# Seven products for eight in a transformer step: layer 1's up projection by Strassen's algorithm

## The chip, the cores and the metric

The kernel runs on one core of a Trainium2 chip. The metric is the device time in microseconds; the time before is the median of three runs. Beside the runs there is one profiled execution, whose trace gives the rows below.

## The reference, cut to what matters

Two layers of a decoder are run once over a prompt of 512 tokens and a sample group of 8 x 4 tokens, 544 columns in all. Layer 0 mixes by a Conformer convolution, layer 1 by a state-space layer; each layer then has cross-attention to a memory and an MLP with squared relu. The change is in the MLP of layer 1 and in what stands at its two ends.

```
def _sqrelu_mlp(xn, w_up, w_down):          # w_up (1024, 4096), w_down (4096, 1024)
    h = jax.nn.relu(jnp.einsum('bld,df->blf', xn, w_up))
    return jnp.einsum('blf,fd->bld', h * h, w_down)
...
    x = x + _sqrelu_mlp(_rmsnorm(x, p['norm_ffn'][i]), p['mlp_w_up'][i], p['mlp_w_down'][i])
y = _rmsnorm(x, p['norm_final'])
```

All inputs and outputs are float32.

## The kernel before, in words

The residual stream lies in eight tiles `X[k]` of 128 features by 544 columns. A float32 product is made of three products of reduced-precision parts (`float32r`): each operand is split into a high part, rounded by ScalarE (a copy), and a low part, the difference, made by VectorE. `split` does so for activations, `prep_block` (line 163) for a weight block of 128 x 1024; the three passes are high by high, low by high and high by low. Each pass of one 128 x 128 weight tile runs over the 544 columns in two matmuls of 272 (`gemm`, line 193, matmul at line 208).

The whole trunk is a list of `Step`s. `run` (line 137) goes through it, and each engine gets its instructions in the order in which the code issues them. Ahead of a step, `run` asks for weight blocks (512 KB each) on SP's queue into the staging tiles `wst`, up to `ahead` blocks in advance, and prepares the parts of blocks to come in the three tiles `whl`. PSUM's first six banks serve as three pairs (`mm`, handed out by `ring`), the last two as `aux`.

In layer 1, `att_layer` ends with the output projection: `ofirst` and `ofin` run the products of output tile o, `oend` adds them to `X[o]` and splits the normed tile into `xf` (`norm_in`). The root mean square is not applied there: it is applied, squared, to the results of the down products (`rb`).

`mlp_layer` works by halves of the 4096 middle features. `up(o)` makes one middle tile from one weight block, 48 matmuls, then relu and square on ScalarE and the split into a high and a low tile, of which VectorE makes the low one. After 16 such tiles, `dn(half, o, c)` makes the eight output tiles, two weight blocks each, scales them by `rb` and adds them to `X[o]` (lines 1085 and 1086). In the second half the squares for the final norm are summed as well. The last output tile is made in `finish`, by halves of the columns, so that the final norm of the first half runs beside the products of the second.

Of the kernel before, what the change touches and what calls it, by code (L numbers as in the profile page):

```python
# [57 lines left out]
class Trunk:  # L58
    NST, NHL, NSLOT = 4, 3, 48
# [12 lines left out]
    def __init__(self, nc, tc, pool, psum, I, O):  # L72
# [10 lines left out]
        self.whl = deque(t(f"whl{i}", 2, 1024) for i in range(self.NHL))  # L83
        self.acc = t("acc", T)
        self.rb = t("rb", T)
        self.tmps = deque(t(f"tmp{i}", T) for i in range(2))
        self.accs = t("accs", 1, 128)
# [263 lines left out]
    def start(self):  # L351
# [46 lines left out]
        self.ahead = self.NST - 1  # L398
# [97 lines left out]
    def conv_layer(self):  # L496
# [72 lines left out]
        def end():  # L569
            self.ahead = self.NST  # L570
            self.unhold(self.vb)
# [218 lines left out]
    def att_layer(self, L, bg):  # L790
# [225 lines left out]
        def ofirst():  # L1016
            for k in (6, 7):
# [22 lines left out]
    def mlp_layer(self, L, after, bg):  # L1040
# [54 lines left out]
        for half in range(2):  # L1095
            self.steps += [up(16 * half + i) for i in range(16)]
            last = L == half == 1
            self.steps += [dn(half, o, c) for o in range(8 - last) for c in range(2)]
            if last:
                self.steps.append(Step(lambda: self.finish(M["h"]), [("dn", 1, 7, c) for c in (2, 3)]))  # L1100


    def finish(self, hs):
        nc, V = self.nc, self.nc.vector
        k = KT - 1
        col = lambda t, c: t[:, c * HALF : c * HALF + HALF]
        taus = lambda v, c: [v[:, f, :, 2 * c : 2 * c + 2] for f in range(2)]
        rows = lambda t: t.rearrange("p (j r) -> p j r", r=32)[:, :, :8].rearrange("p j (f t) -> p f j t", f=2)
        ps = [self.ring(self.mm)[:, 0, :HALF] for _ in range(2)]
        sq, own = self.slot(), self.slot()[:, :128]  # L1110
        xs = [self.slot() for _ in range(KT)]
        nc.gpsimd.memset(own, 0.0)  # L1112
        seq = [(c, i, wi, xi) for c, g in ((0, range(8)), (1, range(7)), (1, (7,)))
               for wi, xi in ((0, 0), (1, 0), (0, 1)) for i in g]

        def products(c, a=0, b=len(seq)):
            for n, (half, i, wi, xi) in enumerate(seq):
                if a <= n < b:
                    nc.tensor.matmul(ps[c], self.w8(("dn", 1, k, 2 + half), i)[wi], col(hs[8 * half + i][xi].bitcast(F32R), c),
                                     start=n == 0, stop=n == len(seq) - 1)  # L1120
# [9 lines left out]
        def others():  # L1130

            for f in range(2):
                V.tensor_copy(rows(self.accs[:, 0])[:, f], self.smp(self.acc)[:, f])
            for c in range(2):
# [39 lines left out]
        for _ in r0:  # L1174
            pass
# [673 lines left out]
```

## Time and profile before

| | |
|---|---|
| median of three runs | 1566.04 us (1563.89 to 1566.91) |
| the profiled execution | 1566.66 us, span in the trace 1564.9 us |
| TensorE busy | 1521.7 us, 97% of the span |
| VectorE busy | 897.2 us, 57% |
| ScalarE busy | 620.9 us, 40% |
| mean granted TensorE clock | 0.99 |
| layer 1's MLP without the closing step | 1163.7 to 1536.3 us of the span |

Busy time of an engine is the time in which one of its instructions runs; matmuls are pipelined, so that a busy TensorE says that matmuls follow each other, not that each is at its fastest. [...]

### The profile page before, as it was taken

Reading aid. Unit: us, or ns where it says so; the run is one execution under the profiler, and the core shown is the slowest. Engines: PE = TensorE matmul, PEld = TensorE weight load, DVE = VectorE, ACT = ScalarE, POOL = GpSimd, SP = SyncE. Lnnn points to the kernel's source line nnn. Section 1 sums busy time; section 2 is a strip of 40 time slices with the busy share of each in tenths; the row PEclk is TensorE's granted clock in tenths of the full one; section 3 lists DMA queues with packets and bytes.
Section 4 is the critical chain, followed back from the end, with each engine's and each line's share of the span. In section 5 each row is a group of like instructions: output and inputs, shape, how many; then the busy total and the mean of one; then the engine's idle time right before and its main releaser. Section 6 shows DMA issues by size and latency. Waiting matters only on the chain.

```text
span 1564.9 us, 29123 instructions
## 1 busy us (share of the span) xinstructions
PE 1521.7 (97%) x12129; PEld 1475.6 (94%) x12129; DVE 897.2 (57%) x1771; ACT 620.9 (40%) x1090; POOL 195.2 (12%) x155
## 2 busy tenths in 40 slices
PE   8999989999999999999999999999999999999996
PEld 8999869988999999999998899988899999999996
DVE  6997876444577666666757954454453333332334
ACT  6121354333445433665434443343435421244222
POOL 2445561000000000000104840000000000000001
PEclk9999989999999999999999999999999999999998
DMA  7433433663322444444588965355322222223211
GB/s 274 121 96 97 145 105 122 232 212 122 110 81 91 143 132 132 132 132 139 177 271 253 322 190 188 116 197 197 129 86 95 81 95 94 83 81 95 88 62 58
DMA packets 90804, 218.18 MB, mean 139 GB/s; under 512 B 12304, under 2 KB 42784, under 8 KB 86576
## 3 DMA queue, kind: packets, MB, share of 16 engines
q1 hardware_dynamic: 87440, 211.06, 41.2%
q10 hardware_dynamic: 3168, 5.18, 0.9%
q8 instruction: 95, 1.56, 0.4%
q14 instruction: 37, 0.30, 0.1%
q0 software_dynamic: 64, 0.08, 0.0%
HBM read 186.48 MB, written 29.80 MB: 138 GB/s over the span
## 4 chain that ended last, share of the span: by engine, by line
PE 81%; DVE 11%; DMA 3%; issue 1%; POOL 1%; ACT 1%; SPq 0%; DVEq 0%; POOLq 0%; ACTq 0%
PE banks L208 68%; DVE banks L695 2%; PE banks L460 2%; DMA arena_att<-in_kc 2%; PE banks L885 2%; PE banks L220 1%; DVE whl L170 1%; PE banks L869 1%; PE banks L675 1%; PE banks L443 1%; PE banks L949 1%; DVE banks L1577 1%; POOL arena_mem L648 1%; DMA arena_s<-tab 1%; PE banks L280 1%
## 5 line engine op out<-in xcount | busy, mean ns | idle before, releaser
L208 PE MATMUL banks<-slot,whl 128*128 128x272 f32 x9240 | 1178.0, 289 | 3.3 <-ACT slot L134 2.0
L208 PEld LDWEIGHTS banks<-slot,whl 128*128 128x128 f32 x9240 | 1167.0, 188 | 7.9 <-issue 4.1
L170 DVE TENSOR_TENSOR whl<-wst,whl 128x1024 fp32r<-128x1024 f32 x213 | 263.9, 1242 | 158.0 <-ACT whl L134 153.8
L134 ACT ACTIVATE whl<-wst 128x1024 fp32r<-128x1024 f32 x232 | 243.7, 1053 | 176.4 <-PE banks L208 105.1
L243 DVE TENSOR_TENSOR slot<-tmp,slot 128x544 fp32r<-128x544 f32 x64 | 46.4, 726 | 164.4 <-ACT slot L134 164.4
L134 ACT ACTIVATE slot<-banks 128x512 fp32r<-128x512 f32 (+7 forms) x132 | 60.4, 481 | 139.2 <-PE banks L208 42.0
L134 ACT ACTIVATE tmp<-banks 128x544 f32<-128x544 f32 x64 | 40.0, 625 | 178.1 <-PE banks L208 178.1
L134 ACT ACTIVATE slot<-x,vec 128x544 fp32r<-128x544 f32 (+2 forms) x49 | 35.0, 736 | 115.9 <-DVE x L1013 47.3
L1085 DVE TENSOR_TENSOR tmp<-banks,rb 128x544 f32<-128x544 f32 x31 | 22.5, 724 | 83.3 <-PE banks L208 83.2
L695 DVE SCALAR_TENSOR_TENSOR banks<-slot,vec,banks 128x512 f32<-128x512 f32 x90 | 67.9, 754 | 2.6
L1112 POOL MEMSET slot<- 128x128 f32 x1 | 0.2, 206 | 525.7 <-PE banks L208 525.7
L134 ACT ACTIVATE tmp<-x 128x544 f32<-128x544 f32 x41 | 26.6, 648 | 86.3 <-DVE x L1086 71.8
L675 PE MATMUL banks<-slot,arena_mem 128*128 128x128 f32 (+2 forms) x360 | 46.1, 285 | 7.2 <-POOL arena_mem L648 4.0
L170 POOL TENSOR_TENSOR whl<-wst,whl 128x1024 fp32r<-128x1024 f32 x19 | 46.2, 2437 | 55.5 <-ACT whl L134 55.5
L418 POOL TENSOR_TENSOR slot<-slot,slot 128x512 fp32r<-128x512 f32 x4 | 6.1, 1563 | 371.4 <-ACT slot L134 371.4
L675 PEld LDWEIGHTS banks<-slot,arena_mem 128*128 128x128 f32 x360 | 44.2, 200 | 8.0 <-POOL arena_mem L648 4.6
L648 POOL TENSOR_TENSOR arena_mem<-istk,slot 128x1152 f32<-128x1152 f32 x20 | 46.1, 2307 | 31.4 <-PE banks L675 27.9
L246 DVE SCALAR_TENSOR_TENSOR slot<-x,vec,slot 128x544 fp32r<-128x544 f32 x40 | 30.9, 784 | 27.0 <-ACT slot L134 26.2
L134 ACT ACTIVATE arena_prep<-arena_prep 64x64 f32<-64x64 f32 (+4 forms) x176 | 43.6, 260 | 2.8 <-DVE arena_prep L1362 1.2
L134 ACT ACTIVATE slot<-tmp 128x544 fp32r<-128x544 f32 x64 | 42.2, 660 | 2.0
L134 ACT ACTIVATE tmp<-tmp 128x544 f32<-128x544 f32 x64 | 42.2, 659 | 2.0
L134 ACT ACTIVATE slot<-banks,sm_nb,sm_rs 128x256 f32<-128x256 f32 x40 | 22.0, 563 | 43.5 <-DVE sm_nb L891 43.5
(238 smaller groups left out, 1344.3 us busy)
## 6 DMA issues: line engine op xcount, KB each, us to landing
wst<-in_w SPq DMA_DIRECT2D x231, 512.0 KB, 3.5
arena_att<-in_kc SPq DMA_DIRECT2D x16, 1024.0 KB, 7.0
arena_att<-in_vc SPq DMA_DIRECT2D x16, 1024.0 KB, 6.4
tab<-arena_prep SPq DMA_DIRECT2D x24, 512.0 KB, 5.3
arena_s<-tab SPq DMA_DIRECT2D x8, 768.0 KB, 5.6
arena_s<-tab SPq DMA_DIRECT2D x8, 512.0 KB, 6.6
arena_s<-tab SPq DMA_DIRECT2D x12, 256.0 KB, 5.7
x<-in_x SPq DMA_DIRECT2D x8, 272.0 KB, 6.0
```

What stands on the lines that cost most here:

```text
L134: self.nc.scalar.activation(out, in_, func, **kw)
L170: eng.tensor_sub(t[:, 1].bitcast(F32R), src, t[:, 0])
L208: self.nc.tensor.matmul(ps[:, c, :HALF], w, x[:, c * HALF : c * HALF + HALF], start=first and n == 0, stop=last and n == len(seq) - 1)
L220: self.nc.tensor.matmul(ps[:, c, :HALF], self.w8(b, kt)[wi], rhs[kt][xi].bitcast(F32R)[:, c * HALF : c * HALF + HALF], start=first and kt ...
L243: self.nc.vector.tensor_sub(l.bitcast(F32R), src_h if src_l is None else src_l, h)
L246: self.nc.vector.scalar_tensor_tensor(l.bitcast(F32R), src_h, scale, h, op0=ALU.mult, op1=ALU.subtract)
L460: nc.tensor.matmul(ps[m], self.memt(2 * kp + k2, xi)[:, m * 128 : m * 128 + 128], t[:, wi, k2 * 512 : k2 * 512 + 512], start=kp == 0 and k ...
L648: nc.gpsimd.tensor_mul(mat(n).rearrange("p (n c) -> p n c", n=36), self.istk.unsqueeze(1).to_broadcast([P, 36, 32]), tp(t)[:, c * 36 : c * ...
L675: nc.tensor.matmul(o[:, s:], mat(n)[:, s * 128 : s * 128 + 128], x[:, : 128 - s], start=s == 0, stop=s == 8)
L695: nc.vector.scalar_tensor_tensor(A, win(k), w(k), A, op0=ALU.mult, op1=ALU.add)
L885: nc.tensor.matmul(o, qs[qi], ks[ki], start=e == 0 and i == 0, stop=e == 1 and i == 2)
L1085: nc.vector.tensor_mul(self.c2(t), self.psv(ps), self.c2(self.rb))
```

## The change

Of the 32 middle tiles of layer 1, the first two are made as before (`plain`). The others are made in 15 pairs by Strassen's algorithm in Winograd's form. The two tiles of a pair, the even and odd feature tiles of the input, and the two halves of the 544 columns are the three ways in which a pair's product is cut in two. In place of eight block products there are seven, each of twelve matmuls of 272 columns into a bank of its own (`product`). Four are products of sums of weights (s1, s2, s3 and m) and four of sums of activations (T, t2, t3 and t4); three products have a sum on both sides. The sums of activations, the forms, are made once, in `seven_forms`, while the output projection runs. The sums of weights are made pair by pair in `us_make`, and the seven results are put together by VectorE out of PSUM into the two tiles of the pair (`head`, `rest`, `late`). `late` of a pair stands between `head` and `rest` of the next one.

The parts of weights lie in a ring of ten tiles of 128 x 2 x 512, made of the arena and the three `whl` tiles; `us_take` makes parts up to ten ahead of the one that is used. The staging ring `wst` has six tiles instead of four in the whole kernel, with the lead of four kept elsewhere (`AHEAD`). The middle tiles are worked by quarters: four pairs (in the first quarter the plain tiles and three pairs), then eight output tiles with one weight block each. The last two output tiles, not one, are made in `finish` by halves of the columns. The host lays out the up blocks of layer 1 so that a block holds what a pair's sums add. The scratch for software DMA descriptors is set to 4096.

```diff
-    NST, NHL, NSLOT = 4, 3, 48
+    NST, NHL, NSLOT, AHEAD = 6, 3, 48, 4
...
             self.norm_in(o, V_FFN0 if L == 0 else V_FFN1, self.xf)
+            if L and o % 2:
+                self.seven_forms(o // 2)
...
                 oend(o, ps)
+                if L and o > 4:
+                    self.us_make(2 * (o - 4))
...
+    def seven_forms(self, j):
+        V = self.nc.vector
+        e, f, F, G = self.raws
+        for x, k in ((e, 2 * j), (f, 2 * j + 1)):
+            self.act(x, self.X[k], AF.Copy, scale=self.v(V_FFN1 + k))
+        lo, hi = slice(0, HALF), slice(HALF, T)
+        V.tensor_sub(F[:, lo], e[:, lo], e[:, hi])
+        V.tensor_sub(F[:, hi], e[:, hi], f[:, hi])
+        V.tensor_add(G[:, lo], f[:, hi], F[:, lo])
+        V.tensor_sub(G[:, hi], f[:, lo], G[:, lo])
+        for x, names in ((F, ("T", "t3")), (G, ("t2", "t4"))):
+            h, l = self.slot(), self.slot()
+            self.split(h, l, x)
...
+    def us_make(self, upto):
+        V, S = self.nc.vector, self.sums
+        self.us_load()
+        while self.nu < min(upto, len(self.uitems)):
+            kind, g, half = self.uitems[self.nu]
...
+            if kind == "s2":
+                V.tensor_add(S["s1"], c, d)
+                V.tensor_add(S["s2"], S["s1"], a)
+            elif kind == "s3":
+                V.tensor_add(S["s3"], c, a)
...
+            u = self.uring[self.nu % self.NU]
+            self.act(u[:, 0].bitcast(F32R), src, AF.Copy)
+            V.tensor_sub(u[:, 1].bitcast(F32R), src, u[:, 0])
+            if kind == "s3":
+                V.tensor_add(S["m"], S["s2"], b)
+            self.nu += 1
+            self.us_load()
...
+        def product(form):
+            u, = self.us_take()
+            M["n"] = M.get("n", 0) + 1
+            bank = self.banks[:, M["n"] % 6, :HALF]
+            x = M["forms"][form]
+            for n, (wi, xi) in enumerate(passes):
+                for k in range(4):
+                    nc.tensor.matmul(bank, u[:, wi, k * 128 : k * 128 + 128], x[k][xi].bitcast(F32R),
+                                     start=n == k == 0, stop=n == 2 and k == 3)
+            return bank
...
+        def hidden(r, o):
+            self.act(r, r, AF.Square)
+            h, l = self.slot(), self.slot()
+            self.split(h, l, r)
+            M["h"][o % 8] = (h, l)
...
+            def head():
+                st["p"] = self.p1[p % 2]
+                self.act(st["p"], product("B11"), AF.Copy)
+                V.tensor_sub(e, st["p"], product("t2"))
+
+            def late():
+                r = st["r"]
+                V.tensor_add(r[0][:, hi], f, product("B22"))
+                self.act(r[0][:, hi], r[0][:, hi], AF.Relu)
+                hidden(r[0], 2 * p)
+                V.tensor_add(r[1][:, lo], r[1][:, lo], product("t4"))
+                self.act(r[1], r[1], AF.Relu)
+                hidden(r[1], 2 * p + 1)
+            st["late"] = late
+
+            def rest():
+                r = st["r"] = [rtile(), rtile()]
+                V.tensor_add(f, e, product("T"))
+                V.tensor_add(r[0][:, lo], st["p"], product("B21"))
+                self.act(r[0][:, lo], r[0][:, lo], AF.Relu)
+                g = product("t3")
+                V.tensor_sub(r[1][:, hi], g, f)
+                V.tensor_sub(r[1][:, lo], g, e)
...
+        def dn(q, o):
+            def fn():
+                ps = self.ring(self.mm)
+                us = self.us_take(2)
+                seq = [(kt, wi, xi) for kts in (range(6), (6, 7)) for wi, xi in passes for kt in kts]
...
+                V.tensor_mul(self.c2(t), self.psv(ps), self.c2(self.rb))
+                V.tensor_add(self.X[o], self.X[o], t)
...
+            for n, p in enumerate(ps):
+                pair(p, ps[n - 1] if n else None, n == len(ps) - 1)
...
+            for o in range(8):
+                items([("w", 0), ("w", 1)], len(self.ublocks), [("dn", 1, o, q)])
+                if q < 3 or o < 6:
+                    S.append(dn(q, o))
+        S.append(Step(lambda: self.finish(M["h"])))
...
         for _ in r0:
             pass
+        sixth(1)
         bcast(0)
         products(1, b)
+        others(1)
         for i in range(self.FINADD):
             out(0, i)
         add(1)
...
-        self.mlp_layer(1, lambda k: self.sumsq(k, self.X[k]), 0)
+        self.seven_layer()
```

`sixth(c)` adds one half of output tile 6 to the residual, squares it, adds the squares to the sum for the final norm and gathers the sample columns; `others(c)` forms the part of the mean square that tile 7 has no share in.

## Rows read from the trace of the kernel before

**Rows 1.** The page: span, busy time by engine, DMA queues, chain by line.
```profile
span 1564.9 us, 29123 instructions
...
PE 1521.7 (97%) x12129; PEld 1475.6 (94%) x12129; DVE 897.2 (57%) x1771; ACT 620.9 (40%) x1090; POOL 195.2 (12%) x155
...
q0 software_dynamic: 64, 0.08, 0.0%
...
PE banks L208 68%; DVE banks L695 2%; PE banks L460 2%; DMA arena_att<-in_kc 2%; PE banks L885 2%; PE banks L220 1%; DVE whl L170 1%; PE banks L869 1%; PE banks L675 1%; PE banks L443 1%; PE banks L949 1%; DVE banks L1577 1%; POOL arena_mem L648 1%; DMA arena_s<-tab 1%; PE banks L280 1%
```

**Rows 2.** Windows: layer 1's MLP by stage (first up, first down, second up).
```profile
core 0: us, PE busy (x) PEld busy (x) DVE busy (x) ACT busy (x) POOL busy (x), PEclk, DMA share, GB/s
1163.70:1261.00 97.30, 97.30 (x777) 97.30 (x776) 32.89 (x49) 45.86 (x65) 0.00 (x0) 1.00 0.27 87
1261.00:1358.00 97.00, 97.00 (x773) 97.00 (x772) 32.20 (x34) 17.92 (x17) 0.00 (x0) 1.00 0.27 88
1358.00:1455.50 97.50, 97.50 (x777) 97.50 (x777) 30.50 (x33) 46.33 (x64) 0.21 (x1) 1.00 0.27 87
```

**Rows 3.** Waits in layer 1's MLP, 1163.7 to 1536.3 us.
```profile
engine line waited for: us in total, times, longest us
...
DVE slot L243 <- ACT slot L134: 124.3, 32, 5.5
...
DVE whl L170 <- ACT whl L134: 63.6, 52, 4.5
```

**Rows 4.** Timeline of one up tile of layer 1, all engines.
```profile
start us, us, engine line op out<-in xcount [idle before <-releaser]
...
1192.55 0.63 ACT L134 ACTIVATE tmp<-banks 128x544 f32<-128x544 f32 x1 [3.08 <-PE banks L208]
1193.21 0.66 ACT L134 ACTIVATE tmp<-tmp 128x544 f32<-128x544 f32 x1
1193.90 0.66 ACT L134 ACTIVATE slot<-tmp 128x544 fp32r<-128x544 f32 x1
1194.46 1.04 ACT L134 ACTIVATE whl<-wst 128x1024 fp32r<-128x1024 f32 x1
1194.59 0.73 DVE L243 TENSOR_TENSOR slot<-tmp,slot 128x544 fp32r<-128x544 f32 x1 [3.87 <-ACT slot L134]
1195.54 1.23 DVE L170 TENSOR_TENSOR whl<-wst,whl 128x1024 fp32r<-128x1024 f32 x1 [0.22 <-ACT whl L134]
...
1198.59 0.63 ACT L134 ACTIVATE tmp<-banks 128x544 f32<-128x544 f32 x1 [3.08 <-PE banks L208]
```

**Rows 5.** Timeline of the closing step: weight loads, last adds.
```profile
1536.31 3.05 PEld L1119 LDWEIGHTS banks<-slot,whl 128*128 128x128 f32 x24
...
1544.32 0.44 DVE L1140 TENSOR_TENSOR tmp<-banks,rb 128x272 f32<-128x272 f32 x1 [2.93 <-PE banks L1119]
1544.79 0.44 DVE L1141 TENSOR_TENSOR x<-x,tmp 128x272 f32<-128x272 f32 x1
1545.27 0.43 ACT L134 ACTIVATE slot<-x 128x272 f32<-128x272 f32 x1 [1.91 <-DVE x L1141]
```

**Rows 6.** Groups of instructions by shape, VectorE, then ScalarE.
```profile
L243 DVE TENSOR_TENSOR slot<-arena_att,slot 128x512 fp32r<-128x512 f32 x8 | 5.0, 684 | 0.0
...
L1140 DVE TENSOR_TENSOR tmp<-banks,rb 128x272 f32<-128x272 f32 x2 | 0.9, 438 | 2.9 <-PE banks L1119 2.9
...
L134 ACT ACTIVATE slot<-slot 128x512 fp32r<-128x512 f32 x4 | 2.2, 616 | 0.0
...
L134 ACT ACTIVATE slot<-x 128x272 f32<-128x272 f32 x2 | 0.9, 430 | 3.6 <-DVE x L1141 3.6
```

**Rows 7.** Timeline of VectorE in the state-space stage.
```profile
847.56 0.67 DVE L1587 TENSOR_TENSOR slot<-banks,arena_s 128x512 f32<-128x512 f32 x1
848.15 0.68 DVE L1588 TENSOR_TENSOR slot<-banks,arena_s 128x512 f32<-128x512 f32 x1
848.75 0.68 DVE L1587 TENSOR_TENSOR slot<-banks,arena_s 128x512 f32<-128x512 f32 x1
```

**Rows 8.** Timeline of TensorE around layer 0's layer norm.
```profile
213.43 3.33 PE L460 MATMUL banks<-whl,arena_mem 128*128 128x512 f32 x7
220.60 1.12 PE L326 MATMUL banks<-ident,sm_y 128*128 128x128 f32 x4 [3.84 <-DVE sm_y L318]
```

**Rows 9.** Windows of 2 us, TensorE and its clock, same place.
```profile
core 0: us, PE busy (x), PEclk, DMA share, GB/s
...
222.00:224.00 2.00, 2.00 (x6) 0.50 0.00 0
224.00:226.00 2.00, 2.00 (x8) 0.73 0.00 0
226.00:228.00 2.00, 2.00 (x17) 1.00 0.00 0
...
230.00:232.00 2.00, 1.68 (x14) 1.00 0.00 0
```

**Rows 10.** DMA issues in layer 1's MLP: line, count, KB, us to landing.
```profile
wst<-in_w SPq DMA_DIRECT2D x58, 512.0 KB, 3.4
```

More of the change, by code (lines that the diff above doesn't have):

```diff
@@ L86, in __init__ @@
         self.tmps = deque(t(f"tmp{i}", T) for i in range(2))
+        self.rts = deque(t(f"rt{i}", T) for i in range(2))
         self.accs = t("accs", 1, 128)
@@ L397, in start @@
         self.tpt = [self.slot() for _ in range((len(self.TOEP) + 2) // 3)]
-        self.ahead = self.NST - 1
+        self.ahead = self.AHEAD - 1
         for n, i in enumerate(self.TOEP):
@@ L569, in end @@
         def end():
-            self.ahead = self.NST
+            self.ahead = self.AHEAD
             self.unhold(self.vb)
@@ L1096, in mlp_layer, with seven_begin @@
             self.steps += [up(16 * half + i) for i in range(16)]
[L1097 to L1100, printed above, removed]
+            self.steps += [dn(half, o, c) for o in range(8) for c in range(2)]
+    NU = 10
+    def seven_begin(self):
+        ar = self.new_arena("mlp1")
+        u = [ar[0][:, i * 1024 : i * 1024 + 1024] for i in range(4)]
+        for t in self.hltiles:
+            f = t.rearrange("p a b -> p (a b)")
+            u += [f[:, i * 1024 : i * 1024 + 1024] for i in range(2)]
+        self.uring = [x.rearrange("p (x n) -> p x n", x=2) for x in u]
+        self.sums = {n: ar[1][:, i * 512 : i * 512 + 512] for i, n in enumerate(("s1", "s2", "s3", "m"))}
+        self.p1 = [ar[1][:, 2048 + i * HALF : 2048 + i * HALF + HALF] for i in range(2)]
+        self.raws = [ar[1][:, i * T : i * T + T] for i in range(4)]
+        self.forms = {n: [] for n in ("T", "t3", "t2", "t4")}
+        self.nu = self.nused = 0
@@ new lines, in seven_forms @@
+    def seven_forms(self, j):
[11 more added lines that the diff above has]
+            self.split(h, l, x)
+            for n, c in zip(names, (lo, hi)):
+                self.forms[n].append((h[:, c], l[:, c]))
@@ new lines, in us_raw, with us_load @@
+    def us_raw(self, g, half):
+        return self.wst[(len(self.flat) + g) % self.NST][:, half * 512 : half * 512 + 512]
+    def us_load(self):
+        while self.nub < len(self.ublocks) and (self.nub < self.NST or self.ulast[self.nub - self.NST] < self.nu):
+            self.nc.sync.dma_start(self.wst[(len(self.flat) + self.nub) % self.NST], self.I["w"][BLOCK[self.ublocks[self.nub]]])
+            self.nub += 1
+    def us_make(self, upto):
[3 more added lines that the diff above has]
+            kind, g, half = self.uitems[self.nu]
+            if kind != "w":
+                a, b, c, d = (self.us_raw(g + x, y) for x, y in ((0, 1), (1, 1), (1, 0), (0, 0)))
+            if kind == "s2":
[3 more added lines that the diff above has]
+                V.tensor_add(S["s3"], c, a)
+            src = self.us_raw(g, half) if kind == "w" else S[kind] if kind in S else {"a": a, "b": b, "c": c, "d": d}[kind]
+            u = self.uring[self.nu % self.NU]
[5 more added lines that the diff above has]
+            self.us_load()
@@ L1105, in finish @@
         k = KT - 1
+        us = self.us_take(4)
         col = lambda t, c: t[:, c * HALF : c * HALF + HALF]
@@ L1164, in finish @@
         products(0, 0, 24)
-        for i in range(k):
+        sixth(0)
+        for i in range(6):
             self.act(xs[i], self.X[i], AF.Copy, scale=self.v(V_FIN + i))
-        others()
         products(0, 24)
+        others(0)
         a, b = self.FINAT
@@ L1517, in stats @@
                 up_fetch(k)
-            self.ahead = self.NST - 1
+            self.ahead = self.AHEAD - 1
         def begin():
@@ L1654, in glu_late @@
         def glu_late():
-            self.ahead = self.NST
+            self.ahead = self.AHEAD
             self.gemm_kt(D["ps"], D["s"], kts=(6, 7), first=False)
@@ L1776, in _layout @@
             t = w[b[3] * 256 : b[3] * 256 + 256, b[2] * 512 : b[2] * 512 + 512].reshape(2, P, 512).transpose(1, 0, 2)
+        elif n == "up" and b[1] == 1:
+            o = b[2] - b[2] % 2
+            x, y = (cols(g["mlp_w_up"][1], i).reshape(P, 4, 2, P) for i in (o, o + 1))
+            t = np.concatenate([y[:, :, 1], x[:, :, 0]] if b[2] == o else [y[:, :, 0], x[:, :, 1]], axis=1)
         elif n == "dn":
```

123 lines of the change are left out of this document (105 added, 18 removed).

## The prediction

> **What bounds the kernel now.** I read the page's header and chain of waits first: TensorE is busy 97% of the span, and one matmul line holds 68% of the chain that ended last [rows 1]. Then I read the stretches of layer 1's MLP: in both halves TensorE is busy in the whole stretch at full clock, VectorE a third of it [rows 2]. The waits of this MLP name no wait of TensorE. They show VectorE waiting 124.3 us, in 32 pieces, for ScalarE's parts of the hidden tiles [rows 3]. TensorE sets the time, and VectorE's pauses are free because it has nothing else to do.
>
> The timeline of one up tile shows what such a pause is. Relu starts at 1192.55, square and copy follow, and VectorE's subtraction starts at 1194.59, 2.04 us after the relu started; only then, behind the pause, comes the next weight block's subtraction [rows 4]. Each engine runs its queue in the order of the code. Relus of successive tiles stand 6.04 us apart [rows 4], so a matmul of 272 columns costs 6.04 / 48 = 0.126 us.
>
> **The gain.** Before, the up products are 32 tiles of 48 matmuls, 1536. After, two plain tiles have 96, and 15 pairs have seven products of 12 matmuls, 1260: 1356 together. The down products stay at 1536. 180 x 0.126 = **22.6 us less TensorE work**. A product takes 1.51 us, a pair 10.6 where two tiles took 12.1. Matmuls with different weights one after the other, as a product has them, keep the pace: in the closing step 24 take 3.05 us of weight loads, 0.127 each [rows 5].
>
> **What VectorE gets to do.** Durations: 0.68 us for 128x512 and 0.44 for 128x272 from PSUM [rows 6], 0.73 for a hidden tile's second part [rows 4]. Operations that wait for nothing follow each other faster than they last: 128x512 ones start at 847.56, 848.15, 848.75, every 0.595 us [rows 7]. So I take 0.09 off each operation that another follows at once: 0.595, 0.35 and 0.635.
>
> A pair has seven subtractions that make weight parts and four sums (s1, s2, s3, m), all 128x512: 11 x 0.595 = 6.5. It has seven operations on halves: 7 x 0.35 = 2.4. Two second parts of hidden tiles: 1.3. That is 10.2 us, already TensorE's 10.6. To it come the pauses in which VectorE waits for ScalarE with nothing to overtake:
>
> - in `late`, after the sum into r0's half: relu of a half 0.43 [rows 6], square 0.66 and copy 0.66 [rows 4], with 0.04 at the changes of engine: 1.85;
> - in `late`, after the sum into r1: relu, square, copy of whole tiles: 2.1;
> - the parts of s2 and s3: a sum, ScalarE's copy (0.62 [rows 6]), the subtraction: 0.7 each.
>
> These are 5.35, and 0.36 for the four operations that now run to their full end. **A full pair is 16.0 us of VectorE's queue against 10.6 of TensorE's, and 12.1 for the two tiles before.** ScalarE has seven copies of 0.62, one of about 0.4, relus of 1.5 and 4 x 0.66: 8.9 us, so it isn't the bound. The seven operations on halves empty the products' banks, and six banks turn: TensorE gets about six products ahead and is then held.
>
> **What the lead covers.** The ring holds ten parts, so a quarter begins with its first nine made while VectorE had time in the down products. A middle quarter is 28 products, 42.3 us on TensorE. On VectorE: a first pair without `late` (9 x 0.595 + 5 x 0.35 + 1.6 = 8.7), three full pairs (48.0), a closing `late` (7.3) make 64.0. Of the sums counted, one s3 and two s2 aren't due, since the last nine parts made are plain weights: 2.0 and 1.6 less, the latter because behind r0's relu the next copy is then waited for (1.1 for 0.7). With 1.8 us until the first product is there, VectorE is done after 62.2. The first down tile can run its first 36 matmuls, then needs the last pair's hidden tiles: it ends at 62.2 + 1.5 = 63.7 instead of 42.3 + 6.0 = 48.3. **Loss 15.4 us in each of three quarters.**
>
> The first quarter has three pairs, 31.7 us on TensorE; VectorE's 48.0 - 3.6 = 44.4. It comes in late. The odd output tiles build the forms (four halves, two second parts and their waits, about 4.9), which with the even tiles just fits: 12.7 against 12.1 us for two. But parts, form and norm of the last tile, and the root's chain fall into the plain tiles: some 21 us in 12.1. I take 7 of that as carried into the first pair. 44.4 + 7 + 1.5 - 37.7 = **15.2**. The four make 61.4 us of stall.
>
> **The clock.** In layer 0's layer norm TensorE stands for 3.84 us and comes back at 220.60 [rows 8]. The granted clock is 0.50 until after 224, 1.00 from 226 on; pauses of a few tenths, around 230, leave it at 1.00 [rows 9]. [...] Each quarter ends in a stall of up to some 10 us, so I take about 4.4 us at half speed behind each: 4 x 2.2 = 8.8. [...]
>
> **The rest.** The last two down tiles end in halves. `sixth(1)` stands on VectorE ahead of the last tile's `add(1)`: two operations of 0.44, a wait for ScalarE's square (0.43), a sum and small copies [rows 5], about 2.0 us on the tail. The DMAs carry the same 64 blocks, 3.4 us each to landing [rows 10], asked for some twelve parts (18 us) ahead: nothing. The ring of six staging buffers with the lead kept at four changes nothing before this MLP; nothing also for the smaller DMA scratch, as the software queue moves 64 packets [rows 1].
>
> **Sum.** -22.6 + 61.4 + 8.8 + 2.0 = +49.6. The profiled execution took 1566.66 us (span 1564.9 and 1.8 around it), 0.6 above the median: 1566.7 + 49.6 = **1616 us**, slower by 3%.
>
> Bounds: if no operation overlaps its follower, a pair costs VectorE 15 x 0.09 = 1.35 more, 20 us in all. If the first down tile must also wait for a bank that the last product's late evacuation holds, its first 36 matmuls no longer cover: 4 x 4.5 = 18. If the clock never falls, 9 less; if the carried lag is nothing, 7 less; if half of the pauses in `late` fall where TensorE hasn't yet run ahead, 15 x 2 = 30 less.
>
> **Rivals.**
>
> - **VectorE keeps up; faster.** If `late`'s pauses and those of s2 and s3 held nothing back, a pair would need 10.2 us there, under 10.6: no stall, 1566.7 - 22.6 + 2.0 = 1546. For it: ten parts of lead, six banks, and a VectorE that is idle for two thirds before [rows 2]. Against: the 2.04 us chain with the weight's subtraction behind it [rows 4]. It decides where a quarter loses under (22.6 - 2.0) / 4 = 5.1 us. Chance 0.13.
> - **Half the pauses hide.** Loss per quarter 5 to 10 us, some clock: 1567 to 1590. Chance 0.13, of which 0.04 within 0.2% of no change (about what a measurement of this kernel can tell from none).
> - **The low clock spreads.** Product waits of 2 to 4 us in the stalled pairs drop the clock there. [...] For it: 3.84 us was enough [rows 8]; against: pauses of tenths were not. Chance 0.09.
> - **The forecast**, 1595 to 1640: 0.65.
>
> The range leaves out the first rival and the worst of the third: 1575 to 1650. Faster 0.13, same 0.04, slower 0.83.
>
> **What would show it.** 180 fewer matmuls. TensorE's busy share in layer 1's up stretches down to about two thirds, named waits of it on VectorE's half operations and on hidden tiles, the longest at each quarter's first down tile. VectorE's queue full or waiting for ScalarE there, with pauses of about 2 us ahead of the hidden tiles' second parts. Down stretches still dense; granted clock under 1.00 behind each stall. I am wrong if pairs stand 10.6 us apart, or if VectorE's subtractions are shorter than 0.6.

## The result, and the profile after

The changed kernel takes 1630.37 us, median of four runs (1629.49 to 1631.36); before took 1565.72 beside it. The ratio is 1.0414, 95% interval 1.0396 to 1.0432: slower by 4.1%. The forecast was 1616, inside its range of 1575 to 1650.

The page of the profiled execution (1630.8 us), beside [rows 1]: span, busy time by engine, the chain that ended last by engine.

```profile
span 1628.9 us, 29336 instructions
...
PE 1523.3 (94%) x11949; PEld 1473.3 (90%) x11949; DVE 1033.4 (63%) x2106; ACT 673.4 (41%) x1247; POOL 193.7 (12%) x155
...
PE 70%; DVE 18%; ACT 6%; issue 3%; DMA 2%; POOL 1%; SPq 0%; DVEq 0%; ACTq 0%; POOLq 0%
```

TensorE has the 180 matmuls less, and is busy 1.6 us longer than before all the same: some of its time is at half clock (a granted clock of 0.50 of full speed, in the windows of 2 us below). VectorE, with 136 us more work, is now 18% of the chain. Windows of layer 1's MLP up to the closing step, of the closing step, and of the pairs of the second quarter, beside [rows 2]:

```profile
core 0: us, PE busy (x) PEld busy (x) DVE busy (x) ACT busy (x) POOL busy (x), PEclk, DMA share, GB/s
1159.91:1599.07 439.16, 378.49 (x2813) 373.71 (x2812) 255.34 (x455) 173.18 (x307) 0.21 (x1) 0.92 0.21 70
1599.07:1628.90 29.83, 17.20 (x128) 16.20 (x126) 17.40 (x64) 8.41 (x17) 4.45 (x5) 0.79 0.23 76
...
1282.91:1345.00 62.09, 50.63 (x368) 49.56 (x367) 40.63 (x76) 32.18 (x59) 0.00 (x0) 0.92 0.30 102
```

In the kernel before, the output projection and the MLP share one matmul line. The column sums of the norm stand behind the 48 matmuls of the first middle tile, so the MLP's first matmul is found by counting back from them; the sum that empties the last output projection's banks starts beside it:

```profile
1154.82 11.87 PE L208 MATMUL banks<-slot,whl 128*128 128x272 f32 x93
1160.68 0.72 DVE L1013 TENSOR_TENSOR x<-x,banks 128x544 f32<-128x544 f32 x1 [1.78 <-PE banks L208]
1166.53 0.95 PE L280 MATMUL banks<-ones,acc 128*128 128x2 f32 x8
...
1536.44 3.15 PE L1119 MATMUL banks<-slot,whl 128*128 128x272 f32 x24
```

That is 1160.48, not 1163.7 as the table of the time before has it. The MLP lasted 376.0 us before (1160.48 to 1536.44) and lasts 439.2 now: +63.2. The closing step is 1.4 us longer, and the MLP begins 0.6 us earlier; together the span's +64.0. Note the third window: TensorE stands for a fifth of it, and VectorE, which holds it up, is itself busy only two thirds of the time. What it does in the rest is what this study is about.

Waits in the MLP, first TensorE's, then VectorE's, beside [rows 3] (line, what it waited for: us in total, times, longest):

```profile
PE banks L1210 <- DVE acc L1247: 18.3, 7, 4.2
PE banks L1297 <- DVE rt L1237: 12.2, 2, 6.3
PE banks L282 <- DVE accs L279: 7.3, 1, 7.3
PE banks L1297 <- DVE rt L1240: 5.9, 2, 3.0
...
DVE slot L245 <- ACT slot L136: 67.6, 32, 7.5
DVE whl L1170 <- ACT whl L136: 21.9, 27, 1.2
DVE arena_mlp L1170 <- ACT arena_mlp L136: 13.0, 17, 1.0
```

Line 1210 holds the products' matmuls, 1297 the down products', 1247, 1237 and 1240 empty the products' banks. TensorE had no named wait here before. VectorE waits for ScalarE 102.5 us in these three rows, 67.6 of them ahead of the hidden tiles' second parts (line 245), the others ahead of weight parts (line 1170).

Timeline of a full pair in the second quarter, from one sum into r0's half (line 1237) to the next:

```profile
1296.33 0.43 DVE L1237 TENSOR_TENSOR rt<-acc,banks 128x272 f32<-128x272 f32 x1
1298.64 0.72 DVE L245 TENSOR_TENSOR slot<-rt,slot 128x544 fp32r<-128x544 f32 x1 [1.88 <-ACT slot L136]
1299.28 0.68 DVE L1170 TENSOR_TENSOR whl<-wst,whl 128x512 fp32r<-128x512 f32 x1
1299.88 0.43 DVE L1240 TENSOR_TENSOR rt<-rt,banks 128x272 f32<-128x272 f32 x1
1302.42 0.73 DVE L245 TENSOR_TENSOR slot<-rt,slot 128x544 fp32r<-128x544 f32 x1 [2.11 <-ACT slot L136]
1303.06 0.68 DVE L1166 TENSOR_TENSOR arena_mlp<-wst,wst 128x512 f32<-128x512 f32 x1
1304.50 0.69 DVE L1170 TENSOR_TENSOR whl<-arena_mlp,whl 128x512 fp32r<-128x512 f32 x1 [0.76 <-ACT whl L136]
...
1305.71 0.43 DVE L1247 TENSOR_TENSOR acc<-acc,banks 128x272 f32<-128x272 f32 x1
...
1309.18 0.69 DVE L1170 TENSOR_TENSOR arena_mlp<-arena_mlp,arena_mlp 128x512 fp32r<-128x512 f32 x1 [0.76 <-ACT arena_mlp L136]
...
1312.63 0.43 DVE L1237 TENSOR_TENSOR rt<-acc,banks 128x272 f32<-128x272 f32 x1
```

The pair takes VectorE 16.30 us; the forecast was 16.0. The pauses are 1.88, 2.11, 0.76 and 0.76, together 5.51, forecast 5.35. The sum at 1305.71, which frees a bank, could have run much earlier: by the matmuls in the trace its product ended at 1298.2. It stands behind two pauses, 2.11 and 0.76.

Timeline of the plain tiles, TensorE and VectorE:

```profile
1159.91 6.21 PE L1280 MATMUL banks<-slot,arena_mlp 128*128 128x272 f32 x48
...
1165.96 0.95 PE L282 MATMUL banks<-ones,acc 128*128 128x2 f32 x8
...
1173.95 0.24 DVE L279 COPY accs<-acc 128x16 f32<-128x16 f32 x2
1174.25 0.59 PE L282 MATMUL banks<-ones,accs 128*128 128x2 f32 x2 [7.35 <-DVE accs L279]
...
1174.70 8.45 PE L1280 MATMUL banks<-slot,arena_mlp 128*128 128x272 f32 x48
...
1185.22 0.73 DVE L245 TENSOR_TENSOR slot<-rt,slot 128x544 fp32r<-128x544 f32 x1 [7.47 <-ACT slot L136]
```

The column sums for the norm need two small copies on VectorE, and these stand behind six weight parts and their sums: TensorE waits 7.35 us in the middle of a step that has nothing to do with them, and its next 48 matmuls take 8.45 us where the first 48 took 6.21.

TensorE's return after the end of the first quarter, and windows of 2 us there, beside [rows 9]:

```profile
1228.94 0.59 PE L1297 MATMUL banks<-slot,whl 128*128 128x272 f32 x1 [5.92 <-DVE rt L1237]
1232.49 12.73 PE L1297 MATMUL banks<-slot,whl 128*128 128x272 f32 x81 [2.95 <-DVE rt L1240]
...
1232.00:1234.00 2.00, 1.51 (x6) 1.51 (x7) 0.43 (x2) 1.47 (x3) 0.00 (x0) 0.50 0.02 4
1234.00:1236.00 2.00, 2.00 (x10) 2.00 (x10) 1.33 (x2) 1.02 (x2) 0.00 (x0) 0.50 0.00 0
1236.00:1238.00 2.00, 2.00 (x12) 2.00 (x11) 0.00 (x0) 0.00 (x0) 0.00 (x0) 0.59 0.55 137
1238.00:1240.00 2.00, 2.00 (x18) 2.00 (x17) 0.00 (x0) 0.63 (x1) 0.00 (x0) 1.00 0.31 125
```

Behind the two stalls the clock stands at 0.50 until after 1236, and 81 matmuls take 12.73 us where full pace would be 10.2.

**The balance.** Before, 2976 matmuls and the norm's 15 small ones, which take 1.5 us, filled the 376.0 us without a stall: 0.1258 each. At that pace the 732, 720, 720 and 624 matmuls of the four quarters would last 93.6 (with the 1.5), 90.6, 90.6 and 78.5 us. By the trace they last 123.0, 107.8, 109.2 and 99.2.

| us | forecast | measured |
|---|---|---|
| 180 matmuls fewer | -22.6 | -22.6 |
| first quarter, stall and clock | 15.2 + 2.2 | 29.4 |
| second quarter | 15.4 + 2.2 | 17.2 |
| third quarter | 15.4 + 2.2 | 18.6 |
| fourth quarter | 15.4 + 2.2 | 20.7 |
| closing step | 2.0 | 1.4 |
| ahead of the MLP | 0 | -0.6 |
| sum | 49.6 | 64.1 |

### The profile page after: what moved, and what is told of

Same layout as the page of the kernel before. It is cut to its first block, busy times and chain, and to the rows that moved or that the text cites. A ratio compares the mean times of both kernels' runs of the same rounds, so it can differ in the third digit from the quotient of the medians.

```text
span 1628.9 us, 29336 instructions
## 1 busy us (share of the span) xinstructions
PE 1523.3 (94%) x11949; PEld 1473.3 (90%) x11949; DVE 1033.4 (63%) x2106; ACT 673.4 (41%) x1247; POOL 193.7 (12%) x155
## 4 chain that ended last, share of the span: by engine, by line
PE 70%; DVE 18%; ACT 6%; issue 3%; DMA 2%; POOL 1%; SPq 0%; DVEq 0%; ACTq 0%; POOLq 0%
PE banks L210 43%; PE banks L1297 11%; DVE banks L697 2%; PE banks L1210 2%; ACT rt L136 2%; ACT slot L136 2%; DVE whl L1170 2%; PE banks L462 1%; PE banks L951 1%; PE banks L887 1%; PE banks L445 1%; DMA wst<-in_w 1%; PE banks L677 1%; DVE whl L172 1%; DVE arena_mlp L1170 1%
## 5 line engine op out<-in xcount | busy, mean ns | idle before, releaser
L210 PE MATMUL banks<-slot,whl 128*128 128x272 f32 x6264 | 803.4, 289 | 5.8 <-ACT slot L136 2.4
L210 PEld LDWEIGHTS banks<-slot,whl 128*128 128x128 f32 x6264 | 792.4, 188 | 10.8 <-ACT slot L136 4.3
L136 ACT ACTIVATE whl<-wst 128x1024 fp32r<-128x1024 f32 (+1 forms) x236 | 217.8, 929 | 118.3 <-issue 37.3
L172 DVE TENSOR_TENSOR whl<-wst,whl 128x1024 fp32r<-128x1024 f32 x149 | 187.0, 1259 | 97.5 <-ACT whl L136 94.8
L1297 PE MATMUL banks<-slot,whl 128*128 128x272 f32 x912 | 130.2, 302 | 28.4 <-DVE rt L1237 12.2
L1297 PEld LDWEIGHTS banks<-slot,whl 128*128 128x128 f32 x912 | 125.3, 201 | 30.4 <-DVE rt L1237 12.6
L1210 PE MATMUL banks<-slot,whl 128*128 128x272 f32 x756 | 102.9, 297 | 13.1 <-DVE acc L1247 9.5
L1210 PEld LDWEIGHTS banks<-slot,whl 128*128 128x128 f32 x756 | 100.1, 196 | 14.7 <-issue 10.3
L1210 PE MATMUL banks<-slot,arena_mlp 128*128 128x272 f32 x504 | 70.4, 301 | 10.0 <-DVE acc L1247 8.8
L1210 PEld LDWEIGHTS banks<-slot,arena_mlp 128*128 128x128 f32 x504 | 68.7, 201 | 10.7 <-issue 9.4
L136 ACT ACTIVATE rt<-rt 128x544 f32<-128x544 f32 (+1 forms) x77 | 43.9, 570 | 75.7 <-DVE rt L1237 30.4
L1297 PE MATMUL banks<-slot,arena_mlp 128*128 128x272 f32 x528 | 72.2, 289 | 1.8 <-DVE acc L1247 1.8
L1297 PEld LDWEIGHTS banks<-slot,arena_mlp 128*128 128x128 f32 x528 | 68.7, 189 | 2.2 <-DVE acc L1247 2.1
L245 DVE TENSOR_TENSOR slot<-rt,slot 128x544 fp32r<-128x544 f32 x32 | 23.2, 726 | 67.6 <-ACT slot L136 67.6
L136 ACT ACTIVATE tmp<-banks 128x544 f32<-128x544 f32 x32 | 20.0, 624 | 76.4 <-PE banks L210 76.4
```

What stands on the lines that cost most here:

```text
L136: self.nc.scalar.activation(out, in_, func, **kw)
L172: eng.tensor_sub(t[:, 1].bitcast(F32R), src, t[:, 0])
L210: self.nc.tensor.matmul(ps[:, c, :HALF], w, x[:, c * HALF : c * HALF + HALF], start=first and n == 0, stop=last and n == len(seq) - 1)
L245: self.nc.vector.tensor_sub(l.bitcast(F32R), src_h if src_l is None else src_l, h)
L1210: nc.tensor.matmul(bank, u[:, wi, k * 128 : k * 128 + 128], x[k][xi].bitcast(F32R), start=n == k == 0, stop=n == 2 and k == 3)
L1297: nc.tensor.matmul(ps[:, c, :HALF], us[kt // 4][:, wi, kt % 4 * 128 : kt % 4 * 128 + 128], M["h"][kt][xi].bitcast(F32R)[:, c * HALF : c * ...
```

## The experiments

The theory: VectorE has work enough for 10.2 us a pair, and it is the order of its queue, with pauses behind ScalarE in it, that makes 16. Rivals: the ring and the quarters cost the time themselves; VectorE's volume of work is the bound; the half clock is a cause and not a consequence. All ratios are to the kernel before in runs on the same chip. The changed kernel itself was not run again there; its ratio's interval (1.0396 to 1.0432) overlaps those of the runs below that come within a few us of it, so differences of that size are read from the traces, one execution each. Lengths of the quarters by trace, in us:

| kernel | first | second | third | fourth | sum |
|---|---|---|---|---|---|
| without a stall | 93.6 | 90.6 | 90.6 | 78.5 | 353.3 |
| the changed kernel | 123.0 | 107.8 | 109.2 | 99.2 | 439.2 |
| second parts deferred | 123.1 | 107.5 | 107.5 | 98.3 | 436.4 |
| copies ahead | 113.9 | 102.1 | 101.8 | 93.5 | 411.3 |
| both | 106.6 | 91.4 | 90.3 | 79.1 | 367.4 |
| all | 98.9 | 90.3 | 90.2 | 79.3 | 358.7 |
| statistics first | 117.5 | 107.8 | 109.1 | 99.1 | 433.4 |
| clock kept, 48 | 123.5 | 107.9 | 106.8 | 98.8 | 437.0 |
| clock kept, sized | 120.8 | 107.8 | 107.4 | 97.3 | 433.3 |
| bank choice alone | 120.0 | 108.3 | 109.1 | 98.2 | 435.6 |

### The quarters and the ring without Strassen's products

All tiles are made as plain ones, two from four parts, 48 matmuls each; the forms and the sums of weights are gone, the ring, the quarters, the six staging tiles and the closing step stay.

```diff
-            if L and o % 2:
-                self.seven_forms(o // 2)
...
         for q in range(4):
...
-            for n, p in enumerate(ps):
-                pair(p, ps[n - 1] if n else None, n == len(ps) - 1)
+            for p in range(4 * q, 4 * q + 4):
+                items([("a", 0), ("b", 0), ("c", 0), ("d", 0)], len(self.ublocks), [("up", 1, 2 * p), ("up", 1, 2 * p + 1)])
+                S.append(plain(p))
```

> The ring of parts, the six staging tiles, the quarters and the closing by two tiles are kept, but all 32 middle tiles are made by eight block products, as the first two are; no forms, no sums. TensorE has its 1536 up matmuls again. Theory (the seven products' assembly on VectorE makes the loss): VectorE has about 8 us for two tiles' 12.1, no stalls: 1566 to 1575 us, as before the change plus some 2 us of closing. Rival (ring and quarters cost time themselves): 1580 us or more.

Measured: 1564.78 us (1562.65 to 1567.19, ten runs), ratio 0.9987 (0.9974 to 1.0). By trace the MLP lasts 375.5 us, 376.0 before. The rebuilding around the products costs nothing that can be measured; the loss belongs to the seven products and what VectorE does for them.

### VectorE's second parts of hidden tiles, deferred

The subtraction that waits for relu, square and copy is put behind the next bank's sum.

```diff
-            self.split(h, l, r)
+            self.act(h.bitcast(F32R), r, AF.Copy)
             M["h"][o % 8] = (h, l)
+            low = lambda: V.tensor_sub(l.bitcast(F32R), r, h)
+            if defer:
+                lows.append(low)
+            else:
+                low()
...
                 V.tensor_add(f, e, product("T"))
+                flush()
```

> The changed kernel with one thing moved: the subtraction that makes a hidden tile's low part isn't issued right behind its sums, but after the next product's result has been added (at a quarter's end, after the last tile's copy). Every instruction is the same, only VectorE's order differs. Theory (VectorE's queue with its pauses is the bound, 16.0 us a pair, 3.95 of it the pauses in late): a pair falls to about 12.0 us against TensorE's 10.6, the quarters lose 0 to 3 us in place of 17 to 20, the first quarter keeps its long wait for the statistics: 1562 to 1580 us. Rival (the volume of VectorE's work, or the low clock, is the bound): the work is the same, 1622 to 1635 us.

Measured: 1627.67 us (1627.38 to 1629.19), ratio 1.0388 (1.0366 to 1.0409): next to nothing. The time is the rival's, but not for its reason, as the timeline shows. Timeline of VectorE and ScalarE in this kernel:

```profile
1311.88 0.43 DVE L1248 TENSOR_TENSOR rt<-acc,banks 128x272 f32<-128x272 f32 x1
1312.34 1.12 ACT L136 ACTIVATE rt<-rt 128x272 f32<-128x272 f32 x2 [2.11 <-DVE rt L1248]
1313.50 0.66 ACT L136 ACTIVATE slot<-rt 128x544 fp32r<-128x544 f32 x1
1314.07 0.61 ACT L136 ACTIVATE whl<-wst 128x512 fp32r<-128x512 f32 x1
1314.71 0.69 DVE L1170 TENSOR_TENSOR whl<-wst,whl 128x512 fp32r<-128x512 f32 x1 [2.40 <-ACT whl L136]
```

The pause hasn't gone. The next operation of VectorE is a weight part's subtraction, and it needs ScalarE's copy of that weight, which stands in ScalarE's queue behind relu, square and copy of the hidden tile. VectorE waits 2.40 us here in place of 1.88. My expectation saw one queue; there are two, and in this timeline each runs in its order. A full pair takes 15.90 us (1295.98 to 1311.88) in place of 16.30.

### The same second parts on GpSimd

```diff
-            self.split(h, l, r)
+            self.act(h.bitcast(F32R), r, AF.Copy)
+            nc.gpsimd.tensor_sub(l.bitcast(F32R), r, h)
```

> The changed kernel with the low part of each hidden tile made by GpSimd in place of VectorE; nothing else. Theory (pauses): VectorE's queue loses two subtractions (1.3 us) and the two pauses before them (3.95): about 10.7 us a pair, so TensorE bounds again: 1558 to 1578 us. Rival (volume): only 1.3 us a pair less work, 15 x 1.3 = 20 us: about 1610 us.

Measured: 1637.58 us (1636.98 to 1640.05), ratio 1.0452 (1.0429 to 1.0475): slower than the change, and outside both expectations. Timeline of GpSimd and VectorE in this kernel:

```profile
1318.41 1.36 POOL L1223 TENSOR_TENSOR slot<-rt,slot 128x544 fp32r<-128x544 f32 x1 [10.41 <-issue]
1318.83 1.48 DVE L1170 TENSOR_TENSOR whl<-wst,whl 128x512 fp32r<-128x512 f32 x1 [2.40 <-ACT whl L136]
...
1322.87 1.33 POOL L1223 TENSOR_TENSOR slot<-rt,slot 128x544 fp32r<-128x544 f32 x1 [3.10 <-ACT slot L136]
1323.35 1.40 DVE L1170 TENSOR_TENSOR whl<-arena_mlp,whl 128x512 fp32r<-128x512 f32 x1 [2.08 <-ACT whl L136]
```

The pause of 2.40 is the same as in the kernel before this, and VectorE's subtraction takes 1.48 and 1.40 us instead of 0.68 while GpSimd's runs. The 1.3 us of work a pair that were taken away come back as 1.5 us in these two subtractions, 0.80 and 0.72 longer, so this run doesn't tell VectorE's volume from its order; it shows that the pause isn't tied to the operation that was moved.

### ScalarE's copies two parts ahead

A weight part's copy is issued on ScalarE two parts before VectorE's subtraction of it; m's sum stands beside s3's.

```diff
+                V.tensor_add(S["m"], S["s2"], b)
+            u = self.uring[self.nu % self.NU]
+            self.act(u[:, 0].bitcast(F32R), self.us_src(self.nu), AF.Copy)
             self.nu += 1
+            self.us_low(self.nu - self.LAG)
...
+    def us_low(self, upto):
+        while self.nlow < upto:
+            u = self.uring[self.nlow % self.NU]
+            self.nc.vector.tensor_sub(u[:, 1].bitcast(F32R), self.us_src(self.nlow), u[:, 0])
+            self.nlow += 1
```

> Only the second half of that: ScalarE's copies two parts ahead, m beside s3, the low parts of hidden tiles where they were. Theory: the pauses at s2 and s3 (1.4 us a pair) go, those in late (3.95) stay, a pair falls from 15.7 to about 14.3: some 5 us a quarter, 1604 to 1616 us. If the pauses in late were hidden by something else, it would come out near the run with both, under 1580 us.

Measured: 1601.99 us (1600.98 to 1603.67), ratio 1.0232 (1.0215 to 1.025), a little better than expected. The pauses ahead of weight parts are gone, those in `late` (1.89 and 2.11) remain; a full pair takes 14.64 us.

### Both queues reordered

The two edits together.

> The late low parts as in the first of these runs, and now ScalarE's queue is changed too: ScalarE's copy of a weight part is issued two parts ahead of VectorE's subtraction for the same part, and the sum m is made beside s3. The same instructions, another order. Theory (two queues in order: VectorE's next subtraction stands behind ScalarE's relu, square and copy, because its own copy is queued behind them, so moving the low parts alone moved nothing): now neither waits for the other, a pair needs 10 to 11 us of VectorE against 10.6 of TensorE; the first quarter keeps its wait for the statistics: 1560 to 1578 us. Rival (VectorE's volume of work or the low clock): 1615 to 1630 us.

Measured: 1556.32 us (1554.97 to 1557.8), ratio 0.994 (0.9922 to 0.9957): faster than before. Windows of this kernel over the pairs of the second quarter, and the sum into r0's half of two pairs:

```profile
1267.00:1309.00 42.00, 42.00 (x337) 42.00 (x336) 37.80 (x74) 29.48 (x56) 0.00 (x0) 1.00 0.39 135
...
1277.30 0.44 DVE L1262 TENSOR_TENSOR rt<-acc,banks 128x272 f32<-128x272 f32 x1 [0.41 <-PE banks L1224]
...
1288.45 0.43 DVE L1262 TENSOR_TENSOR rt<-acc,banks 128x272 f32<-128x272 f32 x1
...
1298.33 0.44 DVE L1262 TENSOR_TENSOR rt<-acc,banks 128x272 f32<-128x272 f32 x1
```

TensorE is busy the whole time at full clock. Two pairs take 21.03 us, 10.5 each, and VectorE now waits for TensorE's bank (0.41). The same operations that took 16.30 fit, with 37.80 of 42 us busy. In the sum of the quarters VectorE's order alone was worth 2.8 us, ScalarE's 27.9, both 71.8, 41 more than the two added up: the pauses of `late` go only when both queues let them go. The time lies just under the expected range.

### The statistics ahead of the parts

Six parts are made by then. The last four of the ring's ten are made behind the norm's copies instead of ahead of them.

```diff
-            us = self.us_take(4)
+            us = [self.uring[i].bitcast(F32R) for i in range(4)]
+            self.nused += 4
...
                     self.stat_rsqrt(2)
+                    self.us_make(self.NU)
```

> The changed kernel, but the last four of the first ten weight parts are issued after the first plain tile's statistics in place of ahead of it, so the two small copies that the statistics need are no longer behind them on VectorE. Theory: the wait of 7.35 us in the first plain tile and the half clock behind it (2.2 us) go, and nothing comes back, since VectorE stood idle 7.5 us in the second plain tile: 1619 to 1624 us. Rival: VectorE's work is only moved, and the lag comes back as stall at the first quarter's end: 1628 to 1632 us.

Measured: 1626.54 us (1622.06 to 1627.43), ratio 1.0373 (1.0347 to 1.0399). The stall is 2.89 us instead of 7.35, and the first quarter lasts 117.5 us, 5.5 less; in the medians 3.8, about half of what I expected and between the two expectations. The rival's loss at the quarter's end did not come: the first product starts 5.3 us earlier in the MLP, and the quarter is 5.5 shorter. What is missing was never won, since 2.89 us of the stall are left and the next 48 matmuls still take 7.79 us.

### The clock kept up with added matmuls

48 matmuls into a bank that nothing reads, at the start of each quarter's down products, where TensorE stands anyway.

```diff
+                if o == 0:
+                    w = self.xf[0][0].bitcast(F32R)
+                    for n in range(48):
+                        nc.tensor.matmul(self.aux[1][:, :HALF], w[:, :P], w[:, :HALF], start=True, stop=True)
```

> The changed kernel with 48 matmuls added ahead of each quarter's first down product (6.0 us at full clock), into a bank that nobody reads, while TensorE would stand still there (some 5 to 9 us). Theory: each long stall costs about 2 us of half clock behind it; kept busy, TensorE goes on at full clock: 1621 to 1627 us, and the windows behind the quarters' first down tiles show 1.00. Rival (the clock costs nothing that isn't hidden): 1630 us or more, up to 1640 where the added matmuls stand in the way.

Measured: 1628.45 us (1627.37 to 1632.2), ratio 1.0404 (1.0385 to 1.0424). Inconclusive: some 4 us of stall were left behind the added ones in the first and the fourth quarter, and the clock fell to 0.50 all the same. So a second try has 72, 44, 36 and 74 of them, sized by each quarter's stall (in the third behind the first 36 of the 48 matmuls of its first down tile, where that stall is):

> The changed kernel with matmuls added into a bank that nobody reads, this time as many as fill each quarter's stall by the trace of the changed kernel: 72, 44 and 74 ahead of the first down product of quarters one, two and four (9.1, 5.5 and 9.3 us), 36 ahead of its last twelve matmuls in quarter three. The 48 of the run before left some 5 us of stall behind them, in which the clock fell all the same. Theory: the half clock behind the stalls (114 matmuls in 17.1 us, for instance, where they take 14.3) costs 2 to 2.8 us a quarter, so 1619 to 1625 us. Rival: the end of each quarter is set by VectorE whatever the clock, or the added matmuls overrun: 1628 us or more.

Measured: 1626.81 us (1624.5 to 1628.59), ratio 1.0399 (1.0382 to 1.0417). Windows of this kernel at the place shown above:

```profile
1232.00:1234.00 2.00, 2.00 (x16) 1.79 (x15) 1.52 (x3) 0.97 (x2) 0.00 (x0) 1.00 0.39 156
1234.00:1236.00 2.00, 1.80 (x15) 1.79 (x15) 0.15 (x1) 1.75 (x3) 0.00 (x0) 1.00 0.02 4
```

The clock stays at 1.00 there, and the quarters are 2.2, 0, 1.8 and 1.9 us shorter, 5.9 together by trace (3.6 in the medians, between the two expectations). The half clock behind the quarters' stalls is a consequence of these and worth 5.9 of the 85.9 us that the quarters lose.

### Another bank for the first down tile

It takes the pair of banks that was emptied first.

```diff
-                ps = self.ring(self.mm)
+                ps = self.mmv[(M["n"] + 2) % 6 // 2] if o == 0 else self.ring(self.mm)
+                self.touch(self.mm, ps)
```

> The changed kernel, with only the choice of banks changed: each quarter's first down product goes into the two banks whose results were taken longest ago. Theory: in quarters one, two and four that product stood behind the last pair's late sums because it was given one of their banks, so its first 36 matmuls covered nothing; now they run in the stall (4.5 us each): 1614 to 1622 us. Rival: the first product waits for hidden tiles anyway, 1627 to 1632 us.

Measured: 1627.62 us (1626.62 to 1629.27), ratio 1.0406 (1.039 to 1.0423). TensorE's waits in the MLP of this kernel:

```profile
PE banks L1210 <- DVE acc L1247: 18.5, 7, 4.2
PE banks L1298 <- ACT slot L136: 12.7, 5, 3.3
PE banks L1298 <- DVE acc L1247: 9.5, 4, 2.9
```

The down products no longer wait for the late banks. They still wait for another bank, 9.5 us in four waits, but some 36 matmuls now run before the last stall, and then they wait for the hidden tiles. By trace 3.0 us are won in the first quarter and 1.0 in the last, and 0.5 is lost in the second. The rival expectation held: a wait that ends first gives little.

### All together, and with one part ahead

Both queues, the statistics first and the other bank:

> Both queues reordered, the statistics ahead of the parts, and each quarter's first down product goes into the two banks whose results were taken longest ago. Theory: no stall is left but a few us at the quarters' ends, and TensorE's 22.6 us less work shows: 1548 to 1560 us, faster than before the change. Rival (seven products cost VectorE more than it has): 1580 us or more.

Measured: 1550.42 us (1549.38 to 1551.25, six runs), ratio 0.9903 (0.9888 to 0.9917). This beats both kernels, the one before by 1%. Of TensorE's waits in its MLP these are left:

```profile
PE banks L282 <- DVE accs L279: 2.1, 1, 2.1
PE banks L1328 <- ACT slot L136: 1.5, 1, 1.5
```

The quarters together are 5.4 us above the length without a stall, 5.3 of them in the first. The same kernel with ScalarE's copies one part ahead instead of two:

> The kernel of the last run of the call before (all reorderings), with ScalarE's copies one part ahead of VectorE's subtractions in place of two. Theory: the copy for the subtraction after next still stands behind a relu, square and copy, so some 1 to 1.5 us of each pause in late come back: about 12.5 us a pair, 1562 to 1575 us. Rival (one part is enough): 1548 to 1553 us.

Measured: 1549.46 us (1548.92 to 1551.12), ratio 0.9905 (0.9887 to 0.9922): no difference. I had expected pauses to come back; those that do are 0.25 to 0.89 us, and fit into the 10.6.

### The kernel before with six staging tiles

```diff
-    NST, NHL, NSLOT = 4, 3, 48
+    NST, NHL, NSLOT, AHEAD = 6, 3, 48, 4
...
-    nc = bacc.Bacc("TRN2", target_bir_lowering=False, num_devices=1)
+    nc = bacc.Bacc("TRN2", target_bir_lowering=False, num_devices=1, dynamic_dma_scratch_size=4096)
```

The lead stays four in the places that set it.

> The kernel before, with six staging tiles in place of four, the lead of four blocks kept, and the smaller scratch for software DMA; its MLP is untouched. The changed kernel reaches layer 1's MLP 3.9 us earlier in its trace than the kernel before, which the forecast took for nothing. Theory (the two more staging tiles let loads start earlier where they stood behind a buffer): 1561 to 1564 us, 2 to 4 us faster than before, and the MLP starts near 1160. Rival (it is chance in the DMAs of one execution): 1564 to 1568 us.

Measured: 1564.85 us (1563.49 to 1567.25, eleven runs), ratio 1.0004 (0.9995 to 1.0013). The 3.9 us of the expectation came from the wrong start of the MLP in the trace of before; with 1160.48 the changed kernel is 0.6 us early. In this run's trace the norm's column sums start at 1164.35 us, 2.2 earlier than before (1166.53), and yet the medians are equal. So a shift of that size ahead of the MLP comes and goes between executions, and 0.6 is no effect that these runs could show.

## Why the prediction was right, and what was off

**The gain** is as worked out: 180 matmuls at 0.126 us, and TensorE's pace with different weights one after the other held: with both queues reordered two pairs, 168 matmuls, take 21.03 us, 0.125 each.

**VectorE's 16.0 us a pair** was 16.30, the pauses 5.51 for 5.35. "Each engine runs its queue in the order of the code" was the sentence that carried the forecast, and the two reordered queues show it: the same work without the pauses takes 10.5 us a pair, TensorE's pace. The prediction's first rival, that VectorE keeps up, has the right volume of work, 10.2, and the wrong order. It gave 1546 for that case; with both queues reordered and the first quarter mended 1550.42 was measured.

What the prediction did not see is that a pause of `late` is held twice. It ascribed the pause to the position of the hidden tile's subtraction on VectorE. The copies on ScalarE stand behind relu and square as well: moving VectorE's subtraction alone moves the wait to a weight part (2.40 us for 1.88), and moving ScalarE's copies alone leaves the waits in `late` (1.89 and 2.11). The timelines show both: VectorE pauses 2.11 us, from 1300.31 to 1302.42, ahead of a second part, with the sum of 1305.71 behind it whose product ended at 1298.2; and with the second parts deferred it pauses 2.40 us for a copy that ScalarE starts at 1314.07, behind relu and square (1312.34 to 1313.46) and the copy of the hidden tile (from 1313.50).

**The other three quarters** came out near the forecast: 17.2, 18.6 and 20.7 for 17.6 each. VectorE's last hidden part ends 63.8 to 63.9 us into each by the trace, where the prediction had 62.2. That the second quarter's total fits so well is in part luck: behind its first down tile only 1.0 us was lost, where the prediction put 2.2 of half clock. The fourth, the furthest off, has the longest wait for a product's bank at its first down tile (6.3 in the waits), where the forecast let 36 matmuls run ahead. The prediction had this as a bound of 18 us. The other bank got back 3.6 us over the four quarters: most lay beside the wait for the hidden tiles.

**The step that was mis-sized is the first quarter's carried lag**: "I take 7 of that as carried into the first pair". With its clock the quarter was to lose 17.4 us; it lost 29.4, and these 12.0 are most of the 14.4 from 1616 to 1630.37. The lag did not reach the first pair quietly. VectorE's parts stand ahead of the two copies for the column sums, so that TensorE stalls 7.35 us already in the plain tile and pays 2.2 more at half clock (0.50 from 1174 to 1178): 9.6 us for which the sum has no term. The lag behind it comes on top: from the first product to the end of VectorE's last hidden part it is 52.3 us by trace, 7.9 more than the 44.4 without a lag. So the 7 are there, and the 9.6 were missing. VectorE did not catch up while TensorE ran the second plain tile, for it stands 7.47 us ahead of that tile's second part, with the ring full and four of its ten parts taken by the plain tiles: the first pair starts with six parts made, where the prediction counted nine for a middle quarter. Last, the first down tile ends 5.7 us behind that hidden part, forecast 1.5, because its first 36 matmuls did not run ahead; part of this is the half clock that the forecast counted apart. The experiment with the statistics first bears out the first of these (5.5 us by trace), the one with the other bank the last (3.0); the six parts are read from the timeline and the code and were not tested by themselves.

**The clock**: 4 x 2.2 = 8.8 was forecast; the rows show 2.5 us behind the first quarter's end (81 matmuls in 12.73), and filling the stalls won back 5.9 by trace. The "3.84 us was enough" of the prediction is not what the trace of before shows: by windows of 2 us the clock was at 0.50 from 212 on, behind a wait of 2.59 us that ended at 210.42, and stayed there over the 3.84 us. Nor did the low clock spread over the stalled pairs, the third rival: in the second quarter a stall of 4.14 us, which ends at 1322.59, is followed by 0.50 (1324 to 1326; the first 12 matmuls take 2.75 us), stalls of 0.58 and 1.18 us leave the clock at 1.00 (1304 to 1312), the mean over these pairs is 0.92, and a full pair there is as long as VectorE's 16.30 us.

**The closing step** cost 1.4 us for 2.0. The staging tiles cost nothing, as argued (ratio 1.0004), and no wait of TensorE in the MLP names a DMA.

## What to carry to other kernels

Before moving work from the engine that is the bound to one that looks idle, write down that engine's queue in the order of issue, with every wait in it, and compare the whole length, not the busy time, with the time won. If it is too long, look for the pauses in both queues of a producer and consumer: issue the producer's operation at least one item ahead and put the consumer's behind what is ready, in the same edit: here VectorE's alone won 2.8 us, ScalarE's alone 27.9, and both 71.8. A small operation that the bound engine needs goes ahead of a batch that merely fills a buffer.

## What the hardware showed that I had not expected

VectorE's 128x512 subtraction, which takes 0.68 us here by itself, took 1.48 and 1.40 us when it started 0.42 and 0.48 us behind a 128x544 subtraction on GpSimd. GpSimd's ended at 1319.77 and 1324.20, VectorE's at 1320.31 and 1324.75, 0.54 and 0.55 later. What held VectorE's operation back is not shown.
